# RG-LRU gate weights of a hybrid trunk: eight loads at their uses, or two loads per layer when the mixer's pool opens

## The chip, the core and the metric

The kernel runs on one core of a Trainium2 chip, as one program. Its metric is the device time of one execution in microseconds (us). Five engines work beside each other, each through its own list of instructions in order: TensorE for matrix products (PE in the profile, its weight loads PEld), VectorE (DVE), ScalarE (ACT), GpSimd (POOL) and SyncE (SP), whose list here holds the DMA transfers. Engines wait for each other only through semaphores. Whatever stands behind a waiting instruction on the same engine waits too.

## What is computed

A trunk of two layers works on 640 tokens (128 of context, 512 latent) with 1024 features. Each layer is a mixer and then a convolutional feed-forward network (FFN). The mixer reads one normalised input with three groups of heads: a retention, an SSD (Mamba-2) and an RG-LRU. Their outputs are put side by side and go through one output product, `w_out`. Cut to what the change touches:

```
xl = dwconv(xl, lru_conv_w, lru_conv_b)                 # 256 channels, 4 blocks of 64
def lru_dir(xd, d, h0):                                 # d: direction
    xb = xd.reshape(B, T, LRU_BLOCKS, LRU_BW)
    r = sigmoid(einsum('btnc,ncd->btnd', xb, lru_w_a[d]) + lru_b_a[d])
    i = sigmoid(einsum('btnc,ncd->btnd', xb, lru_w_x[d]) + lru_b_x[d])
    log_a = -LRU_C * r * softplus(-lru_lambda[d])
    return rglru_scan(log_a, i * xd, h0)
hf, lf = lru_dir(xl, 0, ...);  hb, lb = lru_dir(flip(xl), 1, ...)
y_lru = (hf + flip(hb)) * gelu(gl)
out = concat([y_ret, y_ssd, y_lru]) @ w_out
x = x + g1 * out                                        # g1, g2, scales, shifts: silu(c) @ w_ada
x = x + g2 * conv_ffn(modulated_norm(x))
```

The gate weights are `lru_w_a` and `lru_w_x`: for each layer, each half of the channels (`c`) and each direction (`d`) they lie in HBM as one block of 128 x 2 x 128 numbers (128 KB), named `wlru`.

## The kernel before

**Order of the work.** All instructions are written out at build time through a wrapper `Engine` (L167, its call is L175, which is why every row of the profile has that line). The wrapper keeps a `Clock` (L60): an estimate of when each engine, tile and transfer is ready. Cooperative threads (`spawn`, `run_threads`, L324 and L335) are stepped when the clock says that what they wait for is there, and are held back while DVE, ACT or POOL are too far ahead of TensorE in the estimate. So the estimate sets the order in which instructions of all threads are emitted, and that order is then each engine's fixed list. The chip itself goes only by semaphores.

**Main stream.** Products with the big weights are jobs in a fixed order. In layer 0 the mixer's jobs are named l0 v l1 c6 c5 c3 c2 c4 q gl1 k z gl0, then three products g, then the output sweep; in layer 1 they are v l0 c2 c6 c5 c4 c3 l1 q z gl1 k gl0, g three times, output sweep. Here l is the RG-LRU input, v, q, k the retention's, c the columns of the SSD's convolution, z and g gates, gl the RG-LRU gate. Their weights come through `Stream` (L373) as `raw` tiles and are split into a high and a low part (`wh`, `wl`). A product is three matmuls, as `wh,h_hi`, `wl,h_hi`, `wh,h_lo`; with the names swapped (`h_hi,wh`) it is a feature-major one. The output sweep has 128x512 matmuls, its input `h_hi`, `h_lo` is filled by transposes (`ident,tok`, `ident,C456`), a gain on DVE and splits on ACT and DVE.

**Fillers.** `Ada` (L597) computes the modulation in units of two 32x512 matmuls (`araw,csil`). Each half of a unit's weights is a transfer of 512 KB (`araw`). A unit is emitted in `run` (L349) when TensorE has nothing else in the estimate, or when its phase is due. A new `araw` load waits for matmuls on the tile that it overwrites.

**The RG-LRU thread.** `lru` (L787) takes per direction the tile `wg`, starts its transfer on SP, and issues for each of two gates two matmuls (128x258 and 128x384, `X,wg`), sigmoids on ACT, tanh, exp, square root, a scan on DVE, and a store of one column, `out_lru`. The next direction begins behind that store. `lru_run` (L1304) starts it per half of the channels.

**The SSD threads.** `dt_run` (L1351) makes the decays of a tile (`ssd_decay`, L894: two loads `tok<-cTd`, twelve DVE steps of 128x128, an exponential on ACT, a product on POOL). `outs` (L1389) then waits for them and does `ssd_out`, `ssd_norm` and `ssd_turn` (matmuls `C`, `pv,C`, `xs,tok`, then the transposes `ident,C456`). The output sweep is a job behind a condition that all tiles of the SSD are done (`S["done"]`).

**The pool.** `xbc_then` (L1309) opens the mixer's pool `fb` with the first column of the convolution. The tiles of the mixer, `wg` among them, are taken from it.

Of the kernel before, what the change touches and what calls it, by code (L numbers as in the profile page):

```python
# [9 lines left out]
F32 = mybir.dt.float32  # L10
F32R = mybir.dt.float32r
AF = mybir.ActivationFunctionType
ALU = mybir.AluOpType
# [5 lines left out]
NRAW = 2  # L19
# [40 lines left out]
class Clock:  # L60
    """estimated times of the engines, for the order in which instructions are emitted"""

# [9 lines left out]
    def windows(self, t):  # L72
        """the tensor engine's clock: how busy the last window was sets the rate of the next"""
        while t >= (self.win + 1) * HAM:
            u = self.busy / HAM
            self.cold = u < 0.85 if self.cold else u < 0.33
            self.busy = 0.0
            self.win += 1
# [32 lines left out]
    def free(self, n):  # L111
        """when the last user of a tile is done"""
        return max([r for r in self.read.get(n, {}).values()] + [self.ready.get(n, (0.0,))[0]])
# [20 lines left out]
def tnames(xs):  # L134
    """what the waits go by: tiles, or the rows of the tiles that are worked on in parts"""
    res = []
    for x in xs:
        n = getattr(getattr(x, "tensor", x), "name", None)
        w = ROWS.get(n.rsplit("_", 1)[0]) if n else None
        if w and not n.startswith(SHARED):  # L140
            ap = [(abs(st), c) for st, c in list(x.ap)[1:]]
            o = x.offset
            res += [f"{n}#{r}" for r in range(o // w, (o + sum(st * (c - 1) for st, c in ap)) // w + 1)]
        elif tname(x):
            res.append(n)
    return res


class Slots:
    """a pool whose tiles take over the waits of the tiles that had their place"""  # L150

# [91 lines left out]
def kernel(ctx: ExitStack, tc: tile.TileContext, a: dict, o: dict):  # L243
# [26 lines left out]

    # PSUM tiles and token-major tiles are taken and given back in emission order, so that no engine waits for a later one
    CAPS = {"mm": (MCAP, 512), "at": (TCAP, 512), "tok": (NTOK, 384), "xn": (2, D), "hf": (4, 512)}
# [42 lines left out]

# [1 line left out]
    threads = []  # L317
# [45 lines left out]
    def pick(after=0.0, **cost):  # L363
        """the engine that would be through first"""
        return min(cost, key=lambda e: max(clk.t[e], clk.now() - 1.0, after) + cost[e])

# [1 line left out]
    def slot_free(tag, bufs):  # L368
        """when the next tile of the tag is free"""
        L = strm.names.get(tag, [])  # L370
        return clk.free(L[-bufs]) if len(L) >= bufs else 0.0

    class Stream:  # L373
        """units of the products' weights: loads run NRAW ahead of the splits, splits tn.look ahead of the products"""

# [44 lines left out]

# [1 line left out]
    craw = const.tile([128, 8, 2], F32, name="craw")  # L422
# [8 lines left out]
    def load_x(key, src):  # L431
        """the residual stream stays out of SBUF while the mixer needs the room"""
        pl.enter("xp", key, side="right")
        x[:] = [pl["xp"].tile([128, D], F32, tag=f"x{t}", name="x") for t in range(5)]
        for t in range(5):
            SP.dma_start(x[t], src[t])
# [22 lines left out]
    def softplus(out, xin, n):  # L459
        """max(x, 0) + log1p(exp(-|x|)), log1p through 2 atanh(e / (2 + e))."""  # L460
        e, d, s2, acc = (small(n, f"sp{i}{n}", 1) for i in range(4))
# [23 lines left out]
    def setup():  # L485
        """log-gates of the retention (l, dir, h), softplus(-lambda) (l, dir, chunk), decay tables"""
        spi, spo = small(32, "spi", 1), small(32, "spo", 1)
# [19 lines left out]

# [1 line left out]
    def fm_piece(ps, w, ks, piece, k0=0):  # L509
# [7 lines left out]
    def fm_job(then, rev=False):  # L517
        """feature-major chunk: then(ps) gives the thread that consumes it"""
        ps = yield from get("mm", 2)
        w = ws.take()  # L520
        for n in range(8):
            for piece in range(2):
                fm_piece(ps, w, (7 - n if rev else n,), piece, 7 if rev else 0)
            if n == 7:
                ws.done()
                spawn(consume(then, ps), 0)
            yield
# [4 lines left out]
    def fm_primed(thens):  # L532
        """some chunks, the columns of the first tiles before the others"""
        wps = []
# [26 lines left out]
    def sweep_job(ks, ncol, ah, al, then, ready=None, keep=None):  # L561
        """token-major product over the k's, units of two k's; then(t, ps) consumes tile t"""
        outs = []
# [6 lines left out]
        while n < len(ks):  # L570
# [22 lines left out]
            n += m  # L593
# [1 line left out]
    mods = {}  # L595

    class Ada:  # L597
        """a unit: one k, two slices of 512 of the columns 2048 r .., to rows (32 j + stream)"""

# [18 lines left out]
        def left(self, due):  # L618
            """units up to the round that is due"""
            return max(0, 16 * (1 + ((0, 1), (0, 2), (1, 0), (1, 1), (1, 2)).index(due)) - self.n_run)  # L620

        def run(self):
            """the next unit, if that keeps nobody waiting"""
            if not self.got or clk.ready[tname(self.got[0])][0] > clk.now():
# [57 lines left out]
    def need(due):  # L682
        """the rounds up to this one, done"""
        while ada.left(due):
            if not ada.run():
                yield 1
# [10 lines left out]

# [1 line left out]
    def split(hi, lo, src, eng=None):  # L699
# [68 lines left out]
    def conv(dst, ps, w, right, rel_):  # L768
        """dst[c] = b + sum_j w[j] ps[c + j - 1]"""
        nt = right + 2  # L770
# [14 lines left out]

# [1 line left out]
    def lru(l, c, X, Y, done):  # L787
# [4 lines left out]
        for d in range(2):  # L792
            gates = []
            wg = fb.tile([128, 2, 128], F32, tag="wg", name="wg")
            SP.dma_start(wg, a["wlru"][l, c, :, d])
            yield 1
# [17 lines left out]
            yield  # L814
            DVE.scalar_tensor_tensor(T, r, 1.0, T, ALU.add, ALU.mult)           # 1 - a = (1 + a) tanh
            DVE.scalar_tensor_tensor(r, T, 2.0, T, ALU.subtract, ALU.mult)      # a^2 - 1
            yield
            ACT.activation(r, r, AF.Sqrt, scale=-1.0)
            ACT.activation(T, T, AF.Identity, scale=-1.0, bias=1.0)             # a
            yield  # L820
# [33 lines left out]

# [1 line left out]
    def ssd_dt(l, S):  # L856
        """dt, cumulative log-decays and their exponentials, token-major [128, tile, dir, h]"""
        xb, dt, la = small(60, "dtx", 1), small(60, "dt", 1), small(60, "la", 1)
# [35 lines left out]
    def ssd_decay(l, S, t):  # L894
        """E[g][m, hh, i]: decay both ways, weighted by dt[m]"""
        E = []
# [28 lines left out]
    def ssd_state(l, S, C, t):  # L925
        """token-major xs; the states that the chunk leaves, [n, g, (dir, hh, p)]"""
        bt, *xd = yield from get("tok", 3)
# [104 lines left out]
    def ssd_turn(l, S, t):  # L1032
        """feature-major, with the gain"""
        yt, = yield from get("tok")
# [17 lines left out]

# [1 line left out]
    def ret_tables(l, R):  # L1054
# [12 lines left out]
    def rope_do(raw, t):  # L1067
        """raw -> rotated token-major tile"""
        if t == 0:
# [159 lines left out]

# [1 line left out]
    jobs = []  # L1231
# [23 lines left out]
    def begin_phase(due):  # L1255
        """the modulation that is due at the end of the phase is spread behind its units"""
        nonlocal phase
        phase = {"n": 0, "i": 0, "due": due}
        if due is not None:
            hook(lambda: setattr(ada, "limit", ada.n_run + ada.left(due)))  # L1260
# [15 lines left out]
    def mixer_jobs(l):  # L1276
# [27 lines left out]
        def lru_run(c):  # L1304
            while c > len(st["lru"]):
                yield
            yield from lru(l, c, X[c], Y[c], st["lru"])

        def xbc_then(n, j):  # L1309
            def then(ps, rel_):  # L1310
                while "fb" not in pl.open:
# [3 lines left out]
                    for key in ("st", "gn", "xp"):  # L1315
                        if key in pl.open:
                            pl.exit(key)
                    pl.enter("fb", f"fb{l}")
                    S["C456"] = pl["fb"].tile([128, 3 * NT], F32, tag="C456", name="C456")
                C[n] = S["C456"][:, NT * (n - 4):NT * (n - 3)] if n > 3 else pl["fb"].tile([128, NT], F32, tag=f"C{n}", name="C")  # L1320
# [318 lines left out]

# [1 line left out]
    def start(thens):  # L1641
# [267 lines left out]
```

## Time and profile before

| what | us |
|---|---|
| median of three runs | 1765.45 |
| the runs | 1758.45 to 1767.54 |
| profiled execution: its span, which is all that is given of its own time | 1752.2 |
| TensorE busy in the span | 1661.6 |
| VectorE busy | 1009.3 |
| ScalarE busy | 718.5 |
| GpSimd busy | 537.4 |

The span lies 13.25 below the median of the runs. The profile tells, for every engine, when each instruction ran, how long the engine sat idle before it and what ended that idle time. The stages follow each other: mixer of layer 0 from about 30 to 372 us, FFN of layer 0 from 412 to 870, mixer of layer 1 from about 902 to 1235, FFN of layer 1 from 1275 to 1702.

### The profile page before, as it was taken

The numbers are of one execution on the slowest core, as the hardware profiler recorded it, in microseconds if no ns is written. First come the engines' busy times: TensorE is split into PE (matmuls) and PEld (weight loads), VectorE is DVE, ScalarE is ACT, GpSimd is POOL, SyncE is SP. The second block draws the span as 40 slices with busy tenths as digits, with TensorE's granted clock in tenths as the row PEclk, the third lists the DMA queues.
The fourth block names the chain that finished last, engine by engine and source line by source line (L and its number), as shares of the span: only waits on it lengthen the run. The fifth ranks groups of instructions, "written<-read, shape, count | busy, mean of one in ns | idle before, by whom it ended". The sixth has DMA issues, their size and how long they took to land.

```text
span 1752.2 us, 25505 instructions
## 1 busy us (share of the span) xinstructions
PE 1661.6 (95%) x10192; PEld 1485.5 (85%) x10192; DVE 1009.3 (58%) x1866; ACT 718.5 (41%) x1136; POOL 537.4 (31%) x344
## 2 busy tenths in 40 slices
PE   6897999999999999999999899999899999999997
PEld 5787878768997999799789876887799989998996
DVE  5467987677443344344464779877854434443445
ACT  6466435426332233223274765443453313331333
POOL 1334653322331233123123355442213212321331
PEclk9998999999999999999999999999999999999999
DMA  8424555533223222322533355643122321222222
GB/s 326 121 49 81 128 179 174 187 109 103 73 73 108 64 82 73 96 73 73 180 121 107 75 135 158 181 166 105 60 73 73 87 81 61 73 85 72 73 85 84
DMA packets 62668, 188.63 MB, mean 108 GB/s; under 512 B 9550, under 2 KB 17734, under 8 KB 62550
## 3 DMA queue, kind: packets, MB, share of 16 engines
q1 hardware_dynamic: 62550, 187.01, 34.7%
q8 instruction: 80, 1.31, 0.3%
q14 instruction: 38, 0.31, 0.1%
HBM read 180.46 MB, written 6.52 MB: 107 GB/s over the span
## 4 chain that ended last, share of the span: by engine, by line
PE 72%; DVE 14%; ACT 4%; DMA 4%; issue 3%; POOL 1%; SPq 0%; POOLq 0%; DVEq 0%; ACTq 0%
PE at L175 72%; DVE tok L175 5%; DVE x L175 2%; DMA wg<-in_wlru 2%; DVE gt L175 1%; DVE sp L175 1%; DVE C L175 1%; DMA tok<-cTd 1%; ACT L175 1%; DVE lb L175 1%; ACT xn L175 1%; ACT hf L175 1%; POOL wl L175 1%; DMA araw<-in_w_ada 1%; ACT lb L175 1%
## 5 line engine op out<-in xcount | busy, mean ns | idle before, releaser
L175 POOL TENSOR_TENSOR wl<-raw,wh 128x1024 fp32r<-128x1024 f32 (+3 forms) x167 | 388.3, 2326 | 946.7 <-ACT wh L175 883.2
L175 PE MATMUL at<-h_hi,wh 128*128 128x258 f32 (+2 forms) x1912 | 599.9, 314 | 5.0 <-ACT wh L175 3.9
L175 PE MATMUL at<-h_hi,wl 128*128 128x258 f32 (+2 forms) x1912 | 590.4, 309 | 5.6 <-POOL wl L175 4.8
L175 PE MATMUL at<-h_lo,wh 128*128 128x258 f32 (+2 forms) x1912 | 590.0, 309 | 0.5 <-DVE h_lo L175 0.5
L175 PEld LDWEIGHTS at<-h_hi,wh 128*128 128x128 f32 x1912 | 363.7, 190 | 20.1 <-issue 5.2
L175 PEld LDWEIGHTS at<-h_hi,wl 128*128 128x128 f32 x1912 | 362.8, 190 | 6.9 <-POOL wl L175 5.9
L175 PEld LDWEIGHTS at<-h_lo,wh 128*128 128x128 f32 x1912 | 364.1, 190 | 2.6 <-DVE h_lo L175 0.7
L175 ACT ACTIVATE wh<-raw 128x1024 fp32r<-128x1024 f32 (+3 forms) x210 | 212.7, 1013 | 223.1 <-PE at L175 168.1
L175 DVE SCALAR_TENSOR_TENSOR cv<-at,par,cv 128x258 f32<-128x258 f32 (+1 forms) x352 | 185.9, 550 | 71.4 <-ACT cv L175 59.6
L175 ACT ACTIVATE cv<-at,par 128x258 f32<-128x258 f32 (+1 forms) x130 | 76.5, 601 | 317.4 <-PE at L175 317.4
L175 PE MATMUL at<-wh,h_hi 128*128 128x384 f32 (+2 forms) x480 | 184.9, 385 | 2.3 <-DVE tok L175 1.4
L175 PE MATMUL at<-wl,h_hi 128*128 128x384 f32 (+2 forms) x480 | 172.6, 359 | 2.7 <-POOL wl L175 2.7
L175 PE MATMUL at<-wh,act_hi 128*128 128x512 f32 x440 | 174.3, 396 | 0.0
L175 PE MATMUL at<-wl,act_hi 128*128 128x512 f32 x440 | 173.6, 395 | 0.6 <-POOL wl L175 0.6
L175 PE MATMUL at<-wh,act_lo 128*128 128x512 f32 x440 | 173.4, 394 | 0.0
L175 PE MATMUL at<-wh,h_lo 128*128 128x384 f32 (+2 forms) x480 | 172.5, 359 | 0.0
L175 DVE TENSOR_SCALAR cv<-at,par 128x384 f32<-128x384 f32 x46 | 31.2, 677 | 188.3 <-PE at L175 188.3
L175 DVE TENSOR_TENSOR gt<-at,gate 128x512 f32<-128x512 f32 x100 | 68.4, 684 | 104.2 <-PE at L175 104.2
L175 ACT ACT_TABLE_LOAD x87 | 111.6, 1283 | 21.9 <-PE at L175 13.6
L175 PEld LDWEIGHTS at<-wh,h_hi 128*128 128x128 f32 x480 | 91.3, 190 | 28.4 <-issue 12.6
L175 PEld LDWEIGHTS at<-wh,act_hi 128*128 128x128 f32 x440 | 82.7, 188 | 24.0 <-issue 3.4
L175 PEld LDWEIGHTS at<-wl,h_hi 128*128 128x128 f32 x480 | 91.2, 190 | 12.2 <-POOL wl L175 3.5
(169 smaller groups left out, 1903.1 us busy)
## 6 DMA issues: line engine op xcount, KB each, us to landing
raw<-in_wup SPq DMA_DIRECT2D x88, 512.0 KB, 3.5
araw<-in_w_ada SPq DMA_DIRECT2D x80, 512.0 KB, 4.5
raw<-in_wdn SPq DMA_DIRECT2D x44, 512.0 KB, 3.5
raw<-in_wfm SPq DMA_DIRECT2D x28, 512.0 KB, 3.6
ar<-in_wada SPq DMA_DIRECT2D x16, 512.0 KB, 10.2
tok<-cTd SPq DMA_DIRECT2D x40, 192.0 KB, 4.6
raw<-in_wout SPq DMA_DIRECT2D x14, 512.0 KB, 3.5
x<-in_xin SPq DMA_DIRECT2D x10, 512.0 KB
```

The costliest lines, as they stand in the source:

```text
L175: res = real(*args, **kw)
```

## The change

`lru` no longer takes a tile and starts a transfer per direction. When the pool `fb` opens, one tile of 128 x 2 x 2 x 2 x 128 numbers is taken and two transfers of 256 KB, one for each half of the channels, are started. `lru_run` also waits until that has been written out. Each layer has two transfers in place of four.

```diff
     def lru(l, c, X, Y, done):
         fb = pl["fb"]
...
         for d in range(2):
             gates = []
-            wg = fb.tile([128, 2, 128], F32, tag="wg", name="wg")
-            SP.dma_start(wg, a["wlru"][l, c, :, d])
+            wg = mods["wg", l][:, c, d]
             yield 1
...
         def lru_run(c):
-            while c > len(st["lru"]):
+            while c > len(st["lru"]) or ("wg", l) not in mods:
                 yield
             yield from lru(l, c, X[c], Y[c], st["lru"])
...
                     pl.enter("fb", f"fb{l}")
+                    wg = mods["wg", l] = pl["fb"].tile([128, 2, 2, 2, 128], F32, tag="wg", name="wg")
+                    for c in range(2):
+                        SP.dma_start(wg[:, c], a["wlru"][l, c])
                     S["C456"] = pl["fb"].tile([128, 3 * NT], F32, tag="C456", name="C456")
```

The rest of the diff removes comments. The order of the emitted instructions changes in both mixers, since the estimate no longer has the transfers at their uses.

SP, start of the mixer of layer 0 (`pv` are SSD states, `raw<-in_wvd` weights of v). Before:

```order
L175 DMA araw<-in_w_ada 128x1024 x2
L175 DMA raw<-in_wvd 128x780
L175 DMA pv<-in_sssd 128x192 x4
L175 DMA raw<-in_wvd 128x780
L175 DMA raw<-in_wfm 128x1024
L175 DMA wg<-in_wlru 128x256
L175 DMA raw<-in_wfm 128x1024 x2
L175 DMA out_lru<-Y 128x1
L175 DMA wg<-in_wlru 128x256
```

After:

```order
L175 DMA araw<-in_w_ada 128x1024 x2
L175 DMA wg<-in_wlru 128x512 x2
L175 DMA pv<-in_sssd 128x192 x4
L175 DMA raw<-in_wvd 128x780 x2
L175 DMA raw<-in_wfm 128x1024 x3
L175 DMA out_lru<-Y 128x1
```

The gate weights moved ahead of the second half of the weights of v, and none stands behind an `out_lru` any more.

TensorE, end of the mixer of layer 0, from the last matmuls of the third product g to the first of the output sweep. Before:

```order
L175 MATMUL at<-h_hi,wh 128x258
L175 MATMUL at<-h_lo,wh 128x258
L175 MATMUL at<-h_hi,wl 128x258
L175 MATMUL at<-h_hi,wh 128x384
L175 MATMUL at<-h_lo,wh 128x384
L175 MATMUL at<-h_hi,wl 128x384
L175 MATMUL at<-araw,csil 32x512 x4
L175 MATMUL at<-ident,tok 128x128 x6
L175 MATMUL at<-wh,h_hi 128x512
L175 MATMUL at<-wl,h_hi 128x512
```

After, from the same filler units on (twelve rows; `pv,C` twice, `xs,tok` six times and `ident,C456` three times follow, and then the output sweep):

```order
L175 MATMUL at<-araw,csil 32x512 x4
L175 MATMUL at<-ident,tok 128x128 x9
L175 MATMUL at<-araw,csil 32x512 x10
L175 MATMUL at<-ident,tok 128x128 x3
L175 MATMUL at<-araw,csil 32x512 x2
L175 MATMUL at<-C 128x128 x2
L175 MATMUL at<-pv,C 128x384
L175 MATMUL at<-ident,tok 128x128 x3
L175 MATMUL at<-pv,C 128x384
L175 MATMUL at<-ident,rows 128x128 x4
L175 MATMUL at<-xs,tok 128x64 x6
L175 MATMUL at<-C 128x128 x2
```

The SSD of the last two tiles, three more groups of turns and twelve more filler matmuls moved from between the products to behind the last of them.

TensorE, middle of the mixer of layer 1, between the sweep z and the next feature-major product (`h_hi,wh`). Before:

```order
L175 MATMUL at<-araw,csil 32x512 x4
L175 MATMUL at<-xs,tok 128x64 x6
L175 MATMUL at<-pv,C 128x384
L175 MATMUL at<-xs,tok 128x64 x6
L175 MATMUL at<-araw,csil 32x512 x2
L175 MATMUL at<-ident,C_8205 128x128 x3
L175 MATMUL at<-araw,csil 32x512 x2
L175 MATMUL at<-h_hi,wh 128x258
```

After (six more rows of the same kinds follow, `araw,csil` eight times among them, before `h_hi,wh`):

```order
L175 MATMUL at<-araw,csil 32x512 x4
L175 MATMUL at<-ident,C_8203 128x128 x3
L175 MATMUL at<-xs,tok 128x64 x6
L175 MATMUL at<-ident,tok 128x128 x6
L175 MATMUL at<-ident,C_8203 128x128 x3
L175 MATMUL at<-araw,csil 32x512 x4
L175 MATMUL at<-C 128x128 x2
L175 MATMUL at<-pv,C 128x384
L175 MATMUL at<-ident,rows 128x128 x4
```

Here too filler units and small matmuls of the SSD and the retention stand together, twice as many as before, with no large product between them. On VectorE a block of some hundred instructions of the SSD moves back in layer 0 with them; TensorE has the same number of matmuls as before.

## Rows read from the trace of the kernel before

**Rows 1.** Windows: stretch, its length, then busy us and instructions of PE, PEld, DVE, ACT, POOL; granted clock.
```profile
57.00:90.00 33.00, 25.55 (x122) 23.32 (x121) 8.45 (x12) 15.33 (x20) 10.60 (x5) 0.90 0.39 80
...
120.00:160.00 40.00, 27.76 (x159) 25.62 (x159) 21.29 (x41) 29.93 (x38) 11.61 (x6) 0.83 0.35 54
160.00:200.00 40.00, 38.03 (x220) 33.73 (x219) 37.60 (x74) 24.62 (x49) 27.35 (x33) 1.00 0.49 114
...
275.00:335.00 60.00, 59.69 (x430) 49.47 (x430) 48.96 (x113) 34.37 (x60) 20.27 (x18) 1.00 0.42 137
...
412.00:870.00 458.00, 458.00 (x2781) 421.91 (x2782) 203.31 (x320) 141.19 (x192) 113.89 (x49) 1.00 0.29 93
```

**Rows 2.** Waits of PE over the whole span: us in total, times, longest.
```profile
PE at L175 <- DMA wg<-in_wlru: 21.7, 4, 11.1
```

**Rows 3.** Timeline of PE, gate matmuls: start, us, form, count [idle before <-releaser].
```profile
84.78 2.48 PE L175 MATMUL at<-X,wg 128*128 128x258 f32 x4 [6.94 <-DMA wg<-in_wlru]
...
152.29 4.62 PE L175 MATMUL at<-X,wg 128*128 128x258 f32 x8 [11.07 <-DMA wg<-in_wlru]
...
958.58 1.24 PE L175 MATMUL at<-X,wg 128*128 128x258 f32 x4
...
991.17 2.48 PE L175 MATMUL at<-X,wg 128*128 128x258 f32 x4 [6.14 <-DVE tok L175]
...
1033.83 1.32 PE L175 MATMUL at<-X,wg 128*128 128x258 f32 x4 [3.19 <-DMA wg<-in_wlru]
...
1060.59 2.48 PE L175 MATMUL at<-X,wg 128*128 128x258 f32 x4 [3.75 <-DVE tok L175]
```

**Rows 4.** Timeline of SP's queue: transfers issued at the gates of layer 0 and 1.
```profile
76.27 0.37 SPq L175 DMA_DIRECT2D wg<-in_wlru  x1
...
141.69 0.38 SPq L175 DMA_DIRECT2D wg<-in_wlru  x1
...
983.50 0.38 SPq L175 DMA_DIRECT2D wg<-in_wlru  x1
...
1052.15 0.43 SPq L175 DMA_DIRECT2D wg<-in_wlru  x1
```

**Rows 5.** Timeline of PE where the output sweep of layer 0 begins.
```profile
328.74 1.06 PE L175 MATMUL at<-araw,csil 128*32 128x512 f32 x8
329.74 0.88 PE L175 MATMUL at<-ident,tok 128*128 128x128 f32 x6
330.37 0.48 PE L175 MATMUL at<-wh,h_hi 128*128 128x512 f32 x1
```

**Rows 6.** DVE groups by form, 275 to 372 us: count | busy, mean ns | idle before, releaser.
```profile
L175 DVE TENSOR_TENSOR h_lo<-tok,h_hi 128x384 fp32r<-128x384 f32 x10 | 5.2, 555 | 3.2 <-ACT h_hi L175 3.2
...
L175 DVE SCALAR_TENSOR_TENSOR tok<-at,par,Gs 128x128 f32<-128x128 f32 x15 | 4.3, 344 | 2.2 <-PE at L175 2.2
...
L175 DVE SCALAR_TENSOR_TENSOR tok<-cst,dt,tok 128x128 f32<-128x128 f32 x6 | 2.1, 352 | 0.2
...
L175 DVE TENSOR_SCALAR tok<-cst,dt 128x128 f32<-128x128 f32 x6 | 1.7, 278 | 0.0
...
L175 DVE TENSOR_TENSOR tok<-at,ec 128x192 f32<-128x192 f32 x4 | 1.2, 348 | 0.0
```

**Rows 7.** Timeline of ACT at the end of the mixer of layer 0.
```profile
312.95 1.28 ACT L175 ACT_TABLE_LOAD   x1
...
322.40 0.52 ACT L175 ACTIVATE tok<-tok 128x384 f32<-128x384 f32 x1 [1.82 <-DVE yss L175]
...
328.32 1.02 ACT L175 ACTIVATE Gs<-at 128x258 f32<-128x258 f32 x2 [3.17 <-PE at L175]
329.23 1.54 ACT L175 ACTIVATE h_hi<-Y 128x128 fp32r<-128x128 f32 x4
```

**Rows 8.** DMA issues of 30:375: transfers, KB each, median us to landing.
```profile
araw<-in_w_ada SPq DMA_DIRECT2D x32, 512.0 KB, 4.3
```

**Rows 9.** The same for `araw` in 1040:1130: min, median, max.
```profile
DMA to landing us min/median/max: 3.9/8.7/9.9
```

## The prediction, made before the changed kernel ran

> **What bounds the kernel now.** I read the stretches first. In the FFNs TensorE is busy the whole time, with the other engines at less than half [rows 1]; nothing in the change touches them, and the changed order leaves them as they were. The mixers are different: in 57 to 90 and 120 to 160 us TensorE is busy only 25.55 of 33 and 27.76 of 40 us, while from 160 on it is nearly full, but VectorE is at 37.60 of 40 as well [rows 1]. So the mixer of layer 0 has two nearly full engines, and its order is what lets them run beside each other. From 275 to 335 TensorE is full at 59.69 of 60 and VectorE at 48.96 [rows 1]: there the SSD's VectorE work lies beside the products g.
>
> Then the waits. Four waits of TensorE, 21.7 us, are put down to the gate weights [rows 2]. The timeline places the large ones at 84.78, 152.29 and 1033.83; two more, at 991.17 and 1060.59, are put down to VectorE, yet a `wg` was issued some 8 us before each, as at the others [rows 3, 4]. The five are 6.94 + 11.07 + 6.14 + 3.19 + 3.75 = 31.1 us. After a wait the granted clock is low: the stretches with the long waits have 0.90 and 0.83 [rows 1], and four gate matmuls take 2.48 us, against 1.24 where TensorE had not stopped [rows 3]. Those are the two levels, 1.2 and 2.4 GHz.
>
> **The change, what it removes.** Layer 0: 6.94 + 11.07 + 0.5 (a small first wait, an estimate) = 18.5 us. For the slow matmuls behind, the four at 84.78 lose 1.24 and the eight at 152.29 lose 4.62 - 2.48 = 2.14 [rows 3]; some of the products next to them are slow too, so I take 2.3 and 2.7, an estimate: 5.0. Layer 1: 6.14 + 3.19 + 3.75 = 13.1 us, and 1.24 at 991.17 and at 1060.59 [rows 3] with what follows, taken as 3.2. In all 18.5 + 5.0 + 13.1 + 3.2 = 39.8 us. Four issues fewer on SP, 0.4 us each [rows 4], are worth nothing: SP waits most of the time.
>
> **What it adds at the same places.** The two transfers per layer stand ahead of two weights of v. They are 512 KB in all, as much as one `araw`, which lands in 4.3 us [rows 8]; the bytes move, whenever they do, so I take 0 and a bound of 1.5. They are on time: the first gate matmul is more than 8 us behind. At 152.29 the last of the four gate matmuls also waits for VectorE's convolution, so not all of 11.07 comes back; at 991.17 a VectorE result stands close behind. I take +3 for both, bounds 1 to 5.
>
> **What it moves, layer 0.** This decides. In the new order the SSD of the last two tiles, three groups of turns and twelve filler matmuls stand behind the last product g and ahead of the output sweep. Before, the sweep starts right behind six transposes, without a wait, at 330.37 [rows 5]. Now TensorE stops there for a chain on VectorE. It can't start earlier: the first operations need `h_hi`, and ACT copies that behind the `Gs` of the last product, which waits for TensorE [rows 7]; VectorE goes in order behind. From there to the last turn VectorE has, counted in the new order, 36 decay steps (18 of 0.278 and 18 of 0.352 us: 11.3), 15 gated turns (0.344: 5.2), 24 operations of 128x384 (about 0.55: 13.2), 8 of 128x192 (0.348: 2.8) [rows 6] and some 15 others, an estimate of 5: 37.5 us. Five splits wait about 0.6 us each for ACT's copy (3.2 over the group [rows 6]): 40.5. TensorE's work in that time is 16 fillers of 1.06 / 4, the transposes at 0.88 / 6 [rows 5], small SSD matmuls and the first 12 of the sweep: 4.2 + 3.3 + 2.7 + 2.8 = 13.0, the last two estimates. It is no extra work, it was between the products before. So 40.5 - 13.0 = 27.5 us are new idle time. Low bound: the steps overlap a little and the splits never wait, 35 - 13 = 22. High bound: variance and norm go through ACT, each behind a table load of 1.28 and an activation of 0.5 [rows 7], 3 or 4 times in the chain (some 7 us), and the fillers' loads go one behind the other, four rounds of 4.3 [rows 8] plus matmuls, 20 us, with a VectorE sum behind the last of them: 40. I take 30, near the low end, since most ACT steps fall beside other VectorE work. The clock will be low when the sweep begins, as it was after the waits [rows 3]: +2.5 (0 to 4). Layer 0 together: -23.5 + 2 + 30 + 2.5 = +11.
>
> **Layer 1.** The SSD is done early there, but the new order has two knots. The second gate group of the second half of the channels now stands so that its second matmul waits for a VectorE sum 17 operations back, about 6.4 us of VectorE by the durations of [rows 6], with 2.0 of TensorE beside it: +4.4 (0 to 6). Behind the sweep z, 16 filler matmuls and the small matmuls of three tiles stand without a large product. The next product waits for ACT, which has 7 table loads of 1.28 [rows 7] and some fifteen activations, about 9 + 9 = 18 us, and for three rounds of filler loads, 4.3 to 8.7 us each [rows 8, 9]. TensorE has 11.6 us of work meanwhile (an estimate by the same forms). With rounds of 5 the end comes at 21 us: +9.5; by ACT alone +6; with rounds of 8.7 about +20. Then +2 for the clock and +1 of the 3 above. Layer 1 together: -16.3 + 1 + 4.4 + 9.5 + 2 = +0.6.
>
> **Sum.** +11 + 0.6, so about +12 us. The profiled execution has a span of 1752.2 us, which would become 1764; the median lies 13.25 above the span, and that lies outside what changes, so 1765.45 + 12 = 1777.
>
> **A rule against this.** The trace shows the transfer's own time is not what costs: a first load, with nothing ahead of it, held TensorE half a microsecond; the others were issued only 8 to 11 us ahead of use [rows 3, 4]. The Trainium skill, DMA: Bandwidth & Descriptors, section Rules for kernel authors, says to issue a DMA early, compute, and wait for it late. By that rule alone the sum would end at the removed part, which is the second rival.
>
> **The rivals.**
> The forecast: the two moved knots stall TensorE for 40 us or more; 1777, within 1769 to 1788. Chance 0.45.
> *Even.* The same knots, but each at its low bound: 22 in layer 0, 7 and 2 in layer 1, 3 for the clock, 3 at the old places: 37 - 39.8 = -3, 1762 (1757 to 1769). For it: TensorE waits less in the mixer from 160 on once VectorE has less to do there, 2 us in each of the stretches of 40 [rows 1]. Against it: a VectorE chain of 37 us hardly gets shorter. Chance 0.26.
> *The gain stays, faster.* The old waits go, and the moved SSD still runs beside the products, because VectorE, with the 11 and more us that TensorE no longer wastes, has its inputs early: what is left are 3 us at the old places, so 1765 - 37 = 1728, or up to 1755 if half of the layer 0 stall remains. It decides at the point where VectorE reaches the last gated turn less than 15 us behind the last product g. Against it: in-order engines, and `h_hi` behind the last `Gs` [rows 7]. It is what the rule above gives. Chance 0.12.
> *Far slower.* Both knots go by the fillers' loads: rounds of 8.7 us in layer 1 [rows 9] and the high bound of 40 in layer 0: 40 + 20 + 6 + 6 + 4 - 39.8 = +36, 1802; half of that way 1792. Chance 0.13.
> *It doesn't do what it says.* The gate matmuls wait as long for something else (the convolution, the sigmoids' buffers) and the order matters little: 1765. Chance 0.04.
>
> **How the numbers follow.** About 0.5%, 8.8 us, is what a measurement of this kernel can tell from no change. Faster by more is below 1756.6: the third case and a tail of the second, 0.14. Slower by more is above 1774.3: most of the first and all of the fourth, 0.55. The rest, 0.31, lies between. The range for 8 in 10 leaves out the third case's main part and the far end of the fourth: 1756 to 1794. The likeliest one's own range is 1769 to 1788.
>
> **What the new profile would show.** Right: no wait for `wg` over 1 us; gate matmuls of 1.24 us per four; ahead of the output sweep of layer 0 waits of TensorE on VectorE's `tok` and `C` adding up to some 30 us, with VectorE nearly full and a granted clock below 1; in layer 1 a stretch of some 20 us with TensorE half idle between sweep z and the next product. Wrong: if TensorE stays over 90% busy in the 40 us ahead of the output sweep of layer 0, the step on the moved chain fails and the time is below 1750. If the gate matmuls still wait for more than 2 us, the removed part is too large. If the FFNs' lengths of 458 us [rows 1] change, something happens that this sum does not have.

## The result

The changed kernel took 1777.32 us (median of 4 runs, 1774.38 to 1780.37), the kernel before beside it 1763.93 us: a ratio of 1.0083, 95% interval 1.0061 to 1.0106, so about 13 us slower. Measured twice more, later, it gave 1.0100 (1.0085 to 1.0116) and 1.0077 (1.0054 to 1.0100). The prediction had 1777 us, 12 above the median that it knew.

The waits for the gate weights [rows 2, 3] are gone: the full list of TensorE's waits has no row for `wg` any more. Four gate matmuls take 1.24 us at places like those of [rows 3]:

```profile
75.66 1.24 PE L175 MATMUL at<-X,wg 128*128 128x258 f32 x4
...
1034.57 1.24 PE L175 MATMUL at<-X,wg 128*128 128x258 f32 x4
```

What came in their place is this (waits of PE over the whole span: us, times, longest):

```profile
PE at L175 <- DVE tok L175: 14.8, 7, 6.3
PE at L175 <- DMA araw<-in_w_ada: 13.3, 9, 4.2
PE at L175 <- DVE C L175: 12.8, 5, 5.1
...
PE at L175 <- ACT xs L175: 6.1, 1, 6.1
```

The stretches of [rows 1], with the same columns, and one more, 309.00:353.70, which is the end of layer 0's mixer:

```profile
57.00:90.00 33.00, 33.00 (x184) 30.60 (x183) 11.48 (x18) 26.34 (x41) 14.60 (x7) 1.00 0.48 101
120.00:160.00 40.00, 37.97 (x236) 35.58 (x234) 33.45 (x58) 33.52 (x46) 23.12 (x18) 1.00 0.60 113
160.00:200.00 40.00, 33.89 (x175) 27.17 (x174) 31.95 (x78) 16.82 (x38) 20.97 (x26) 0.87 0.37 106
275.00:335.00 60.00, 47.23 (x322) 33.50 (x320) 45.96 (x106) 22.05 (x36) 13.21 (x14) 0.89 0.40 131
309.00:353.70 44.70, 25.59 (x96) 13.05 (x95) 35.28 (x99) 13.24 (x27) 10.88 (x14) 0.69 0.43 145
426.00:884.00 458.00, 458.00 (x2774) 421.96 (x2772) 201.77 (x319) 140.65 (x192) 112.67 (x47) 1.00 0.29 92
```

The first two stretches are now full or nearly so, where they had 25.55 of 33 and 27.76 of 40 us. From 160 on TensorE is less busy than before, 33.89 against 38.03, and the end of the mixer has the loss: 25.59 busy us of 44.70, VectorE at 35.28, a granted clock of 0.69. The FFN is as full as it was.

Where the end of the mixer goes wrong is read on TensorE's timeline, from the last matmul of the last product g to the first of the output sweep (start, us, form, count, idle before and releaser):

```profile
308.89 0.34 PE L175 MATMUL at<-h_hi,wl 128*128 128x384 f32 x1
...
313.97 1.05 PE L175 MATMUL at<-araw,csil 128*32 128x512 f32 x4 [2.61 <-DMA araw<-in_w_ada]
...
320.45 3.17 PE L175 MATMUL at<-araw,csil 128*32 128x512 f32 x8 [4.18 <-DMA araw<-in_w_ada]
326.00 1.92 PE L175 MATMUL at<-araw,csil 128*32 128x512 f32 x4 [2.38 <-DMA araw<-in_w_ada]
...
335.58 0.53 PE L175 MATMUL at<-ident,tok 128*128 128x128 f32 x3 [2.05 <-DVE tok L175]
...
350.25 2.82 PE L175 MATMUL at<-xs,tok 128*128 128x64 f32 x12 [6.28 <-DVE tok L175]
353.21 0.87 PE L175 MATMUL at<-ident,C 128*128 128x128 f32 x3
353.73 0.78 PE L175 MATMUL at<-wh,h_hi 128*128 128x512 f32 x1
```

The sweep begins 44.84 us behind the last matmul of g; before it was 330.37 - 328.48 = 1.89 us [rows 5]. First TensorE waits for the fillers' loads, then for VectorE. Behind the waits the clock falls to its lower level of 1.2 GHz: four filler matmuls take 1.05 us at 313.97 and 1.92 us at 326.00.

Three rows serve as marks for the layers: the first transposes of the normed residual behind each mixer (`ident,xn`), and the first matmuls of the SSD's cumulative sums in layer 1 (`la,cst`). Before:

```profile
391.12 1.04 PE L175 MATMUL at<-ident,xn 128*128 128x128 f32 x8
...
952.74 0.85 PE L175 MATMUL at<-la,cst 128*128 128x60 f32 x6 [2.12 <-DVE la L175]
...
1248.33 1.09 PE L175 MATMUL at<-ident,xn 128*128 128x128 f32 x8 [1.99 <-DVE xn L175]
```

After:

```profile
403.80 1.09 PE L175 MATMUL at<-ident,xn 128*128 128x128 f32 x8 [0.43 <-DVE xn L175]
...
967.13 0.89 PE L175 MATMUL at<-la,cst 128*128 128x60 f32 x6 [2.12 <-DVE la L175]
...
1273.49 1.09 PE L175 MATMUL at<-ident,xn 128*128 128x128 f32 x8 [0.44 <-DVE xn L175]
```

Layer 0 is 12.7 us longer up to its mark; in the two later traces of the changed kernel it is 11.1 and 9.4 us longer. Layer 1's mixer (from `la,cst` to `ident,xn`) takes 306.4 us against 295.6, so 10.8 longer; in the two later traces it takes 303.2 and 302.2.

### The profile page after: what moved, and what is told of

It reads as the page before. It is cut to its first block, busy times and chain, and to the rows that moved or that the text cites. A ratio compares the mean times of both kernels' runs of the same rounds, so it can differ in the third digit from the quotient of the medians.

```text
span 1778.3 us, 25507 instructions
## 1 busy us (share of the span) xinstructions
PE 1680.5 (95%) x10192; PEld 1500.0 (84%) x10192; DVE 1007.1 (57%) x1862; ACT 727.2 (41%) x1142; POOL 539.4 (30%) x347
## 4 chain that ended last, share of the span: by engine, by line
PE 68%; DVE 9%; ACT 3%; DMA 2%; issue 2%; POOL 1%; POOLq 0%; SPq 0%; DVEq 0%; ACTq 0%
PE at L175 68%; DVE tok L175 2%; DVE x L175 2%; DMA tok<-cTd 1%; DVE gt L175 1%; DVE h_lo L175 1%; ACT xn L175 1%; ACT hf L175 1%; POOL tok L175 1%; DVE sp L175 1%; DMA araw<-in_w_ada 0%; DVE C L175 0%; POOL wl L175 0%; ACT h_hi L175 0%; DVE Y L175 0%
## 5 line engine op out<-in xcount | busy, mean ns | idle before, releaser
L175 POOL TENSOR_TENSOR wl<-raw,wh 128x1024 fp32r<-128x1024 f32 (+2 forms) x170 | 392.9, 2311 | 966.7 <-ACT wh L175 910.1
```

Source lines behind the costliest of these rows:

```text
L175: res = real(*args, **kw)
```

## The experiments

My theory was that the change does two things of nearly equal size and opposite sign: the early loads give back TensorE's waits, and the order that the estimate then writes out costs more than that. The first pair of runs separates the two. The kernels write the order of one version and move the data of the other: `SP.real` starts a transfer that the estimate doesn't see, `SP.account` shows the estimate one that isn't started.

### The old order with the early loads

```diff
             wg = mods["wg", l][:, c, d]
+            SP.account("dma_start", (wg, a["wlru"][l, c, :, d]), {})
...
                     for c in range(2):
-                        SP.dma_start(wg[:, c], a["wlru"][l, c])
+                        SP.real.dma_start(wg[:, c], a["wlru"][l, c])
```

> The order of before on every engine, word for word, with the two early loads per layer in place of the loads at the uses (the estimate still counts the old ones). My theory: the loads alone give the removed part of the sum, 39.8 - 3 = 37 us, less where VectorE is nearly full anyway, so 1727 to 1740 us; the rest of what the change does is the order. Rival (what waited for the weights waits for the convolution or the sigmoids' buffers instead, and the order matters little): 1755 to 1765 us. Both theories: no wait for wg over 1 us.

Measured: 1739.13 us, the kernel before 1755.74 on that chip, ratio 0.9901 (0.9887 to 0.9916). The loads alone are worth 17 us in the old order, half of the 37 that I expected; the time lies in the range that I gave only because the kernel before was also some 10 us faster here than the 1765 us that the range was built on. Layer 0's mark lies at 370.7 us in place of 391.1, and that is the whole gain: layer 1's mixer takes 297.3 us in place of 295.6. A new wait stands there. On SP's queue, around the last store of an end state:

```profile
1063.84 0.81 SPq L175 DMA_DIRECT2D araw<-in_w_ada  x2
1064.74 0.38 SPq L175 DMA_DIRECT2D out_lru<-lb  x1
```

and on TensorE:

```profile
1074.03 1.92 PE L175 MATMUL at<-araw,csil 128*32 128x512 f32 x4 [4.82 <-DMA araw<-in_w_ada]
```

The filler's load beside an `out_lru` is late now, as the gate weights beside an `out_lru` were before. It is the second of the two `araw`, and it stands ahead of the store: it was issued at 1064.26, the store at 1064.74. It took 9.7 us to land (first row); with the store gathered (below) the same load took 4.6 (second row):

```profile
araw<-in_w_ada SPq DMA_DIRECT2D x1, 512.0 KB, 9.7
...
araw<-in_w_ada SPq DMA_DIRECT2D x1, 512.0 KB, 4.6
```

### The new order with the loads at their uses

```diff
-            wg = mods["wg", l][:, c, d]
+            wg = fb.real.tile([128, 2, 128], F32, tag="wgu", name="wgu")
+            SP.real.dma_start(wg, a["wlru"][l, c, :, d])
...
                     for c in range(2):
-                        SP.dma_start(wg[:, c], a["wlru"][l, c])
+                        SP.account("dma_start", (Ghost(f"wg_l{l}", (128, 2, 2, 128)), a["wlru"][l, c]), {})
```

> The order of the changed kernel on every engine, with the four loads per layer at their uses, as before the change. My theory: the order alone costs what the moved knots cost, about 50 us by the sum of the prediction; but some of the waits for the weights fall together with waits that the new order has there anyway, so 1764 + 30 to 50 = 1794 to 1814 us, at least 17 above the changed kernel. Rival (the order matters little, the loads are hidden in this order): 1770 to 1782 us, as the changed kernel.

Measured: 1805.14 us, ratio 1.0283 (1.0268 to 1.0298): the order alone costs 49.4 us. The waits for the weights are back:

```profile
PE at L807 <- DMA wgu<-in_wlru: 29.1, 4, 11.7
```

Layer 0's mark lies at 423.0 us (+31.9), layer 1's mixer takes 316.0 us (+20.4). So the early loads give 1.0283 - 1.0100 = 0.018, some 32 us, in the new order, nearly twice their 17 us in the old one. Both rivals that let the order count for little fall.

### What holds TensorE ahead of the output sweep of layer 0

Two chains run there, the fillers' loads and VectorE's. One kernel takes away the first, the other shortens the second.

```diff
-                SP.dma_start(t, a["w_ada"][l, 128 * k:128 * k + 128, c:c + 1024])
+                src = a["w_ada"][l, 128 * k:128 * k + 128, c:c + 1024]
+                SP.account("dma_start", (t, src), {}) if (l, r) == (0, 2) else SP.dma_start(t, src)
...
+                PE.real.matmul(dst, csil[:, k, :], par[:, 0:512] if (l, r) == (0, 2) else w, **kw)
```

> The changed kernel, but the 16 units of one round of fillers in the mixer of layer 0, which all stand behind the last product g, multiply a resident tile in place of their 16 loads of 512 KB, which are left out (the second gate and scale of layer 0 are not computed rightly). The matmuls stay. The prediction's theory (VectorE's chain of 37 to 40 us holds TensorE ahead of the output sweep): the sweep starts at most 4 us earlier than at 353.73, 1772 to 1778 us. Rival (the fillers' loads, round by round, hold TensorE and through the load queue also VectorE's inputs): the sweep starts 10 to 16 us earlier, 1760 to 1767 us.

One thing in that text is wrong: only eight of the sixteen units stand behind the last product g, the other eight stand between the products. Measured: 1762.71 us, ratio 1.0046 (1.0031 to 1.0061). The sweep begins at 347.72, 6.0 us earlier than 353.73, which lies between the two theories. The time falls into the rival's range, but the kernel before was also 8 us faster here than in the first pair. TensorE's timeline:

```profile
322.08 0.87 PE L175 MATMUL at<-ident,tok 128*128 128x128 f32 x3 [8.44 <-DVE tok L175]
...
344.24 2.83 PE L175 MATMUL at<-xs,tok 128*128 128x64 f32 x12 [8.56 <-DVE tok L175]
...
347.72 0.78 PE L175 MATMUL at<-wh,h_hi 128*128 128x512 f32 x1
```

Without the loads TensorE waits as long, for VectorE alone. The last g begins at 308.48 here, so the sweep begins 39.2 us behind it, against 44.8, 42.8 and 42.8 us in the three traces of the changed kernel. VectorE is busy 33.81 us of this stretch and waits for the copies of ACT, little else:

```profile
308.50:347.70 39.20, 18.99 (x96) 11.21 (x95) 33.81 (x95) 13.12 (x26) 9.91 (x13) 0.76 0.18 65
```

The loads add 4 to 6 us to that, by a way that I hadn't named. In the changed kernel SP's queue reads:

```profile
310.25 12.48 SPq L175 DMA_DIRECT2D araw<-in_w_ada  x5
322.79 0.90 SPq L175 DMA_DIRECT2D tok<-cTd  x2
```

Five `araw` loads stand on SP, each held until its tile is free, and VectorE's next inputs, `tok<-cTd`, behind them. VectorE waits for them, 4.4 us in this trace and 2.4 and 2.2 in the two later ones:

```profile
DVE tok L175 <- DMA tok<-cTd: 4.4, 2, 4.0
```

The other kernel leaves the loads and takes VectorE's work out:

```diff
+            few = l == 0 and (t, g) in ((3, 1), (4, 0), (4, 1))
+            V = Few() if few else DVE
+            if few:
+                DVE.real.tensor_scalar(Eg, R[0], cs[:, t, 0, 0:1], None, ALU.subtract)
...
-                DVE.tensor_scalar(Eg[:, hh, :], R[0][:, hh, :], cs[:, t, 0, h:h + 1], None, ALU.subtract)
+                V.tensor_scalar(Eg[:, hh, :], R[0][:, hh, :], cs[:, t, 0, h:h + 1], None, ALU.subtract)
```

> The changed kernel, but the last three groups of decays of layer 0 (of tiles 3 and 4, behind the last product g) have 2 VectorE steps of 128x384 in place of 12 of 128x128 each (left out: the decays of these groups aren't the right ones). VectorE's work ahead of the output sweep is 3 x (12 x 0.31 - 2 x 0.5) = some 8 us shorter, all loads stay. Theory of VectorE's chain: the sweep starts 6 to 8 us earlier, a ratio of 1.003 to 1.005. Theory of the fillers' loads: VectorE waits longer instead, the sweep starts at most 3 us earlier, 1.0065 to 1.009.

Measured: 1765.88 us, ratio 1.0066 (1.0053 to 1.0079); the changed kernel beside it 1773.26. The last g begins at 307.10:

```profile
341.96 2.82 PE L175 MATMUL at<-xs,tok 128*128 128x64 f32 x12 [5.25 <-DVE tok L175]
...
345.45 0.78 PE L175 MATMUL at<-wh,h_hi 128*128 128x512 f32 x1
```

The sweep begins 38.4 us behind it: of 8 us less VectorE work 4.5 to 6.5 come through; VectorE waits 2.1 us for GpSimd's `C` and 2.0 for TensorE there, which it did not in the first trace of the changed kernel. This lies between the two theories. Together the runs say: VectorE's chain sets the length, some 39 us of it, and the fillers' loads stretch it by holding up its inputs on SP.

### What holds it behind the sweep z of layer 1

TensorE there in the changed kernel, first trace, from the fillers behind the sweep z to the next large product:

```profile
1097.46 1.07 PE L175 MATMUL at<-araw,csil 128*32 128x512 f32 x8
1103.60 0.87 PE L175 MATMUL at<-ident,C 128*128 128x128 f32 x3 [5.08 <-DVE C L175]
...
1114.66 1.05 PE L175 MATMUL at<-araw,csil 128*32 128x512 f32 x4 [1.63 <-DMA araw<-in_w_ada]
...
1120.05 0.52 PE L175 MATMUL at<-ident,C 128*128 128x128 f32 x3 [2.27 <-DVE C L175]
...
1127.79 0.58 PE L175 MATMUL at<-h_hi,wh 128*128 128x258 f32 x1
```

30.3 us, and 1121.06 - 1094.38 = 26.7 in the second trace and 25.7 in the third. The edit is that of the first kernel of the section before, for the rounds of layer 1: `(l, r) in ((1, 1), (1, 2))`.

> The changed kernel, but the two rounds of fillers of layer 1's mixer multiply a resident tile in place of their 32 loads, which are left out (the gates, shift and scale of layer 1 behind it are not computed rightly). The matmuls stay. The prediction's theory (three rounds of filler loads hold TensorE behind the sweep z): the knot of 1098 to 1131 us loses some 9 us, with less traffic around it the mixer of layer 1 is 8 to 12 us shorter than in the changed kernel, a ratio of 1.003 to 1.006. Rival (VectorE's C, which TensorE was seen to wait for there, holds it): under 4 us shorter, 1.008 to 1.010.

Measured: 1765.96 us, ratio 1.0079 (1.0065 to 1.0093). In its trace the knot begins at 1091.15 and ends here:

```profile
1100.12 1.22 PE L175 MATMUL at<-C 128*128 128x128 f32 x4 [3.12 <-ACT tok L175]
...
1110.12 0.39 PE L175 MATMUL at<-h_hi,wh 128*128 128x258 f32 x1
```

19.0 us, 7 to 11 shorter, and layer 1's mixer has 295.8 us. That is what the prediction's theory wants. The ratio is nearer to what the rival wants, though: it can't be told from the changed kernel's 1.0077 to 1.0100. Part of the way is again SP's queue. In the second trace of the changed kernel VectorE stands still there for an input whose load is queued behind four `araw`:

```profile
1110.89 0.29 DVE L175 TENSOR_SCALAR tok<-tok,cs 128x128 f32<-128x128 f32 x1 [4.55 <-DMA tok<-cTd]
```

How many of the 7 to 11 us are the loads' and how many chance stays open in part. In the three kernels whose layer 1 has the instructions of the changed one but for the stores in one of them the same knot took 24.6, 25.7 and 24.4 us, so 5 to 7 us are gained beside these. The length of layer 1's mixer scatters too: it was 298.0, 299.8 and 299.1 us in these three, 2 to 4 us above the 295.8. A third trace of the changed kernel was to tell whether its 303 to 306 is chance:

> The changed kernel a third time, for the length of layer 1's mixer: 306.4 and 303.2 us in its two traces, but 298.0, 299.8 and 299.1 in three kernels that differ from it only in layer 0 or in the stores. If this is chance from run to run, about 298 to 302 is as likely here as 303 to 307; if those kernels really shorten layer 1, it is 303 us or more again.

It came out at 302.2, between the two, and settles nothing. Of the second trace I had expected this:

> The changed kernel once more, so that it stands beside the other runs on their chip, and for a second trace of its layer 1. Expected: a ratio of 1.008 to the kernel before, as measured first. If the length of layer 1's mixer (306.4 us in its first trace, but 298.0 in the run with the resident fillers, whose layer 1 has the same instructions) is a matter of chance from run to run, it comes out between 296 and 308 us here; if the 306.4 is a property of the order, it is 305 to 308 again.

It came out at 303.2 us, with a ratio of 1.0100, so the 306.4 is not a fixed property of the order.

### Why a load at its use came so late

The old order with early loads had pointed to the stores of the end states, `out_lru`: one column, 128 numbers of four bytes in 128 places. Four kernels in the old order. First, loads at their uses and a store of one number:

```diff
-            SP.dma_start(o["lru"][l, d, c], hs[:, e:e + 1])
+            SP.real.dma_start(o["lru"][l, d, c][0:1], hs[0:1, e:e + 1])
+            SP.account("dma_start", (o["lru"][l, d, c], hs[:, e:e + 1]), {})
```

> The kernel before, in its order, but each store of an end state of the RG-LRU writes one number in place of 128 (the other 127 are left out). SP waits as long for the scan. Theory one (the 128 writes of four bytes stand ahead of the gate weights and delay them): the weights are in use 3.5 to 5 us behind their issue in place of 8 to 11, the waits for them fall from 31 to some 8 us, 1738 to 1750 us. Theory two (the weights share the transfer engines with the big loads around them, the store is nothing): the waits stay within 2 us each, 1760 to 1768 us.

Measured: 1731.95 us, ratio 0.9864 (0.9849 to 0.9879). Theory one holds: the number of writes is what delays the weights. The load that was issued at 76.27 and used at 84.78 [rows 3, 4] is issued at 77.61 here and used at 80.53:

```profile
80.53 1.32 PE L175 MATMUL at<-X,wg 128*128 128x258 f32 x4 [1.32 <-DMA wg<-in_wlru]
```

Second, the same store of 128 numbers from another queue:

```diff
-            SP.dma_start(o["lru"][l, d, c], hs[:, e:e + 1])
+            ACT.real.dma_start(o["lru"][l, d, c], hs[:, e:e + 1])
+            SP.account("dma_start", (o["lru"][l, d, c], hs[:, e:e + 1]), {})
```

> The kernel before, in its order, loads at their uses, but the eight stores of 128 single numbers are started by ScalarE's queue in place of SP's. Theory one (what stands behind a store in the same queue waits for its single-number writes): the weights are used 3.5 to 5 us behind their issue, as with the store of one number, a ratio of 0.985 to 0.990 (ScalarE waits for each scan, which costs a little). Theory two (the writes hold up the transfer engines themselves, whichever queue starts them): the waits for the weights stay at two thirds or more, 0.995 to 1.003.

Measured: 1744.99 us, ratio 0.9963 (0.9949 to 0.9976). The queues (packets, MB, share) show the eight stores apart, 144 packets each:

```profile
q10 hardware_dynamic: 1152, 0.00, 0.0%
```

The gate weights are issued at 75.63, the store at 76.41 on ACT's queue, and the weights are used at 79.26:

```profile
79.26 1.32 PE L175 MATMUL at<-X,wg 128*128 128x258 f32 x4 [0.82 <-DMA wg<-in_wlru]
```

This looks like theory one, but the run doesn't part the two. SP no longer waits for the scan that the store needs, so this load and four others of the gate weights now start 0.3 to 5.4 us ahead of the store instead of behind it. What does start behind a store is late, though it stands in the other queue. In layer 1, with a store on ACT's queue at 1069.54, an `araw` load issued on SP at 1073.97 takes 9.1 us to land (first row); in the kernel with the gathered store and loads at their uses (below) the same load, issued at 1068.35, takes 3.9 (second row):

```profile
araw<-in_w_ada SPq DMA_DIRECT2D x1, 512.0 KB, 9.1
...
araw<-in_w_ada SPq DMA_DIRECT2D x1, 512.0 KB, 3.9
```

So it is behind all eight stores: the first load on SP's queue, issued 1.6 to 4.7 us later, takes 6.9 to 9.8 us to land, and the same eight take 2.9 to 3.9 us with the gathered store. A load issued 0.1 us ahead of the store, at 1069.44, is late too, and a filler waits for it:

```profile
1078.48 1.92 PE L175 MATMUL at<-araw,csil 128*32 128x512 f32 x4 [4.08 <-DMA araw<-in_w_ada]
```

So the writes of a store hold up transfers of both queues, as theory two has it, and 0.9963 lies in the range that it gave; its other sign, long waits for the weights themselves, failed because these loads now start ahead. The Trainium skill, DMA: Bandwidth & Descriptors, section Issuing engines are not separate DMA queues, says that transfers run on the same 16 DMA engines and interleave, whichever engine started them. The trace agrees: a store on ACT's queue delays loads on SP's. Layer 0's mark lies at 374.5 us, just where the kernel with the gathered store and loads at their uses has it, so the late loads cost nothing there. Layer 1's mixer has 297.2 us, 10 more than with the gathered store, which is most of the difference.

Third and fourth, a version that leaves nothing out: GpSimd copies each column into one tile, and at the start of layer 1's FFN one transpose and one store of 8 rows of 512 bytes write them all.

```diff
-            SP.dma_start(o["lru"][l, d, c], hs[:, e:e + 1])
+            j = 4 * l + 2 * d + c
+            POOL.real.tensor_copy(ends[:, j:j + 1], hs[:, e:e + 1])
+            SP.account("dma_start", (o["lru"][l, d, c], hs[:, e:e + 1]), {})
...
+    def lru_ends():
+        ps, = yield from get("at")
+        PE.transpose(ps[0:8, 0:128], ends, ident)
...
+        ACT.activation(row, ps[0:8, 0:128], AF.Copy)
...
+        SP.dma_start(o["lru"].rearrange("l d c p o -> (l d c) (p o)"), row)
```

With the early loads:

> The order of before with the two early loads per layer, and the end states of the RG-LRU gathered: GpSimd copies each column of 128 numbers into one tile, and at the start of the FFN of layer 1 one transpose, one copy on ScalarE and one store of 8 rows of 128 numbers write all of them, in place of eight stores of 128 single numbers. Nothing is left out. Theory (the single-number writes hold up whatever is queued behind them, weights of the gates or of the products): faster than with the early loads alone by 8 to 16 us, a ratio of 0.981 to 0.986. Rival (the early loads already take all that the stores cost): 0.989 to 0.992.

Measured: 1726.21 us, ratio 0.9835 (0.9821 to 0.9848). Layer 1's mixer takes 287.1 us, and the filler that waited 4.82 us doesn't wait:

```profile
1066.26 1.05 PE L175 MATMUL at<-araw,csil 128*32 128x512 f32 x4
```

This beats both kernels, by 28.5 us the one before. With the loads at their uses:

> The kernel before, in its order, with the loads at their uses, and the gathered store of the end states. It closes the square of old or early loads with eight stores or one. Theory (the stores alone made the loads at their uses late): within 5 us of the early loads with the gathered store, a ratio of 0.984 to 0.987. Rival (loads at their uses are late also without the stores): 0.990 or more.

Measured: 1728.39 us, ratio 0.9858 (0.9844 to 0.9871). With the stores out of the way the early loads are worth 2 to 4 us (by the medians and by the ratios), hardly more than the intervals tell apart. In the new order:

> The changed kernel with the same gathered store. Theory (the moved knots are what costs, and they are not behind stores): it gains 3 to 8 us over the changed kernel, a ratio of 1.004 to 1.007. Rival (the stores also cause the loss of the new order): 0.99 to 1.0.

Measured: 1767.96 us, ratio 1.0076 (1.0063 to 1.0089), against 1.0077 to 1.0100 without it: at most some 5 us (1773.26 us for the changed kernel beside it). The stores are not what makes the new order slow: with the gathered store and the early loads in both, the new order takes 1767.96 us and the old one 1726.21, measured side by side.

| order, stores of end states | loads at uses | two early loads |
|---|---|---|
| old, eight | 1 | 0.9901 |
| old, gathered | 0.9858 | 0.9835 |
| new, eight | 1.0283 | 1.0083, 1.0100, 1.0077 |
| new, gathered | not run | 1.0076 |

## Why the prediction was right, and where it was not

**The two halves.** The prediction forecast 36.8 us removed and 48.4 us added by the moved work. The runs give two ways from the one kernel to the other. Order first: 49.4 us added, then 32 to 36 taken off by the loads, which fits. Loads first: 17 us taken off, then 31 to 35 added by the order, so both terms are 14 to 20 us too large, and their errors cancel. That the sum of +12 meets +13.4 (+13 to +18 over three measurements) is thus in part luck. In layer 0 the terms fit both ways: the loads alone give -20.4 us (-21.5 forecast), the order alone +31.9 (+32.5 forecast). The misfit lies in layer 1.

**Layer 0, +11 forecast, +12.7, +11.1 and +9.4 in three traces.** The last product g ends 328.48 - 308.89 = 19.6 us earlier, the sweep begins 43.0 us later behind it, and from there to the mark it is 10.7 us shorter: 43.0 - 10.7 = 32.3 for the knot. The 10.7 us correct a statement of the prediction and of the section on the change: the twelve filler matmuls and the three groups of turns did not stand between the products before, but inside the output sweep, from 333.84 on. The VectorE chain of 40.5 us is the 39.2 of the run without loads. What the step had wrong is the content of the wait, as the stretches from the start to the mark show (columns of [rows 1]; the kernel before, the old order with early loads, the changed kernel):

```profile
0.00:391.12 391.12, 343.47 (x2245) 291.37 (x2246) 273.60 (x595) 193.24 (x322) 145.94 (x123) 0.96 0.49 151
...
0.00:370.72 370.72, 338.27 (x2246) 288.01 (x2246) 274.22 (x594) 193.20 (x322) 145.49 (x123) 0.99 0.51 160
...
0.00:403.80 403.80, 351.43 (x2246) 296.94 (x2246) 271.84 (x591) 195.50 (x324) 146.79 (x124) 0.93 0.48 147
```

The loads take off 15.2 us of idle time and 5.2 us of slow matmuls, where the prediction had 16.5 and 5.0. The order then adds 19.9 us of idle time and 13.2 us of slower matmuls, where it had 30 and 2.5: the price of the clock was far too low, and the idle time too high by about as much. It made no difference, since VectorE set the end: without the loads the sweep still starts 39.2 us behind g. The signs that the prediction named for being right came only in part: TensorE's waits for VectorE ahead of the sweep are 8.7 us, not some 30, and the fillers' loads hold it for 10.3. The loads lengthen the knot by 4 to 6 us, in part by way of SP's queue, which the step on the fillers counted only up to TensorE.

**Layer 1, +0.6 forecast, +6.6 to +10.8 in three traces.** Here two terms were mis-sized. The removed part, 16.3 - 1 = 15.3 us, is 316.0 less 302.2 to 306.4, so 10 to 14 by one trace of the one and three of the other. In the old order the early loads give layer 1 nothing at all (+1.7), since other waits stand in their place, among them the 4.82 us for the filler's load, where the prediction had taken 1 us. The moved part, 15.9, is 316.0 - 295.6 = 20.4 with the loads at their uses, and 302.2 to 306.4 less 297.3, so 5 to 9, with the early loads. The gate group's wait is 2.6 us (4.4 forecast), so it is not that. The knot behind the sweep z was forecast to end at 21 us and took 25.7 to 30.3, with the next product held by VectorE's `C` and not by ACT: VectorE's inputs wait on SP behind the fillers' loads. The queue was named for the fillers alone.

**The step from the span to the median.** I put 13.25 us between them outside what changes. That was wrong: the profiled run of the changed kernel took 1780.37 us at a span of 1778.3, 2.1 apart, and the kernel before took 1753 to 1757 us beside the experiments, which fits its span of 1752.2. Three of the four runs of the kernel before that the result rests on (1762.41, 1765.45, 1767.54) lie above all later ones, of which the highest is 1759.39; why, the traces don't show. By the spans alone the change costs 16.6 to 26.1 us; only kernels timed side by side give the 13 to 18.

**Not foreseen:** a wait of 6.11 us for ACT's `xs` at 166.30 in layer 0, the row of 6.1 in the waits above, in the stretch that has 33.89 of 40 us. I had that stretch as unchanged. In the two later traces it is 3.7 and 3.2 us.

**The rivals.** The gain that stays, 1728: it is what the old order has, in kind. With the early loads alone it was 0.9901 of 1765.45, so 1748, not 1728. The rule of the Trainium skill that it stood on (DMA: Bandwidth & Descriptors, Rules for kernel authors: start early, wait late) thus holds as far as the instructions stay where they are, and there for half of the removed part, because other waits then take their place. That the change does nothing fell with the first two runs, and that it goes far slower with the result; of its two times, 1802 and 1792 for half of the way, the second doesn't come out, since half of +36 gives 1783.

## What to carry to other kernels

Where an estimate writes the order, a change of one transfer is two changes: cost the order apart from the transfer, by running each with the other's half held fixed. Before a late load is moved, look at which small writes go out around it, on any queue: here a store of 128 single numbers, and gathering the stores gave 25 us with the loads left where they were. And on a queue that holds transfers which wait for a tile, every transfer behind them waits too, so what VectorE needs should not stand behind the fillers.

## What the runs showed of the hardware

A store of 0.5 KB in 128 pieces of four bytes took 7.4 to 9.0 us to land in the old order with early loads, more than a load of 512 KB of the streamed weights (medians of 3.5 to 4.2 us), and a gate load behind it in the same queue was used 8.5 us after its issue in the kernel before, in place of 2.9 with a store of one number. With the stores on ACT's queue the next load on SP's still took 6.9 to 9.8 us to land, in place of 2.9 to 3.9 with the gathered store. Eight such stores, 4 KB in all, cost 1.4% of the kernel's time (0.9858 without them).
